# GpSimd scales the attention's probabilities, two kept products change places, four loads move behind the gMLP's tables

## The chip, the cores and the metric

The kernel runs on one core of a Trainium2 chip, as one program in one launch. The metric is the device time of one execution in microseconds; less is better. The core's engines work side by side, each through its own queue in order: TensorE (PE, matmuls; PEld, its weight loads), VectorE (DVE), ScalarE (ACT), GpSimd (POOL) and SyncE (SP). Transfers are issued from the queues of SP, ACT and POOL.

## The reference

One layer of a decoder trunk, in float32, with 512 positions and a width of 2048:

```
h = rms_norm(x, norm_g)
q, kv, g_logits, z_a, uv, z_b, merge_logits = split(h @ w_in)     # w_in is 2048 x 10800
o_a = nsa_attention(q, ...) * silu(z_a)           # 16 heads of 64, 4 key/value groups
o_b = spatial_gating(uv, ln_v_g, ln_v_b, sgu_w, sgu_b) * silu(z_b)
g_a, g_b = split(sigmoid(merge_logits))
x = x + (g_a * (o_a @ w_up_a) + g_b * (o_b @ w_up_b)) @ w_out
x = x + sigmoid(x @ w_ple_gate) * (p @ w_ple)
return rms_norm(x, final_g)
```

The attention has three branches, each with its own keys and values and a sigmoid gate per head and position: compressed, selected and windowed. With 512 positions the selection takes all 8 blocks and the window covers everything before the query, so the last two are plain causal attention with a linear bias per head:

```
o = gb[0] * o_c + gb[1] * o_s + gb[2] * o_w        # o_s = softmax(q k_s * scale - slope * distance) v_s
```

`spatial_gating` computes `u * (tril(W_s) LN(v) + b)` in chunks of 128 positions and 8 groups, with `uv = gelu(uv)`; `b` is `sgu_b`, `W_s` is `sgu_w`.

## The kernel before

Every float32 operand of a matmul is split into a high part, a copy rounded by ScalarE (`high`, L156 and L158), and a low part, the rest, by VectorE (`low`, L162 and L164); a product is three matmuls (high by high, high by low, low by high). Weight tiles arrive through SP's queue (`raw`, `b11`, `b12`, `more`) and are split into `hi` and `lo`, or `hs` and `ls`.

A generator `gemm` runs through a list of jobs in order: `pl` (embedding), `kw`, `vw`, `q0`, `q1`, the block jobs `kv`, `u`, `vn`, `zb` and `m0` to `m3`, the `q` and `za` jobs, `ub0`, `ub1`, `ua0`, `ua1`, and then `wo` and `pg`. `fill(n)` lets it issue n more units, `finish(name)` all up to the end of a job. At each step of a job it calls `flush()`, which issues what was deferred, splits weights two steps ahead, and `pop()`, which issues the next items of a list called `background`. So the order of every queue is fixed by the order in which the program issues.

A block job (kind "S") computes a block of output with seven block products, named by digits, instead of eight. They come in the order 1 and 5 in turn, 6 and 3 in turn, 7, 2 and 4 in turn. One step is 12 matmuls. Products 1, 6, 7 and 4 go to one pair of PSUM banks, 5 and 3 to a second, 2 to a third. `evac_quad` empties them: after products 1, 5 and 6 ScalarE copies the pair to two SBUF tiles (`keep`, L635); after 3, 7 and 2 VectorE adds the kept tiles (`keep6`, `keep5`, `keep1`) and `final` is called on the sum; after 4 `final` takes the banks themselves. The tiles come from rings: `s1` has two, `hi` four, `lo` three. In the `ub` jobs `final` multiplies by the gate (L756) and stores the tile to `y_dram` from GpSimd's queue (L763); the tile is free when the store has landed.

The block jobs over `h` need sums of its parts. The "third sums" of product 7 are written to `s3_dram` during the first jobs, and `load_s3` (L1114) brings them with four transfers of 512 KB from GpSimd's queue to the places in `act_h` and `act_l` that product 7 reads. It stands directly behind `finish("q1")`, ahead of the block job `kv`. The first background item of that job is `load` of `sgu_items`: from the same queue it loads `sgu_b` (`bn`, L1123) and `sgu_w` (`wn`, two transfers, L1126), makes a triangular mask (L1128, L1129) and copies `ln_g` and `ln_b` to DRAM (L1132). Five items later TensorE transposes `bn` (`bias`, L1136), then `wn` (L1143).

The attention is software-pipelined over 48 slots: for each of eight pairs of heads (`ft`) two for query block 3, two for block 2 and one each for blocks 1 and 0. In period s the program issues

- `scores(s)`: TensorE multiplies (L1518, L1519); VectorE adds the bias and takes the extreme of each row (L1522); the exponentials with their sums follow on ScalarE, deferred (L1531),
- `weigh(s - 1)`: VectorE inverts the sums (L1540), multiplies by the branch's gate (L1542) and scales the probabilities with the result (L1546), one instruction for each head and branch: two or four, 128 in all,
- `transpose_probs(s - 2)`: TensorE transposes them (L1570), and ScalarE and VectorE split the result into `pth` and `ptl`,
- `values(s - 3)`: TensorE multiplies by the values (L1589, L1590); `fold` adds the halves, the last addition and the product with the gate on GpSimd (L1607, L1609),

with units of the `q` and `za` jobs between them. The compressed branch of a group of heads (`cmp_scores`, `cmp_softmax`, `cmp_weigh`, `cmp_transpose`, `cmp_values`) and transfers on GpSimd's queue (`load_ob`, L1681 to L1684; `add_half`, L1688) are spread over the periods. `evac_za` multiplies by the gate path on GpSimd (L543).

Of the kernel before, what the change touches and what calls it, by code (L numbers as in the profile page):

```python
# [17 lines left out]
ALU = mybir.AluOpType  # L18
# [60 lines left out]
def kernel(ctx: ExitStack, tc: tile.TileContext, x, p, norm_g, w_in,  # L79
                      pe_k, w1_k, w2_k, pe_v, w1_v, w2_v, ln_g, ln_b, sgu_w, sgu_b,  # L80
                      w_up_a, w_up_b, w_out, w_ple, w_ple_gate, final_g, out):
    nc = tc.nc
    x, out = x[0], out[0]
    p = p[0, 0]
    norm_g, w_in, ln_g, ln_b, sgu_w, sgu_b = norm_g[0], w_in[0], ln_g[0], ln_b[0], sgu_w[0], sgu_b[0]
    pe_k, w1_k, w2_k, pe_v, w1_v, w2_v = pe_k[0], w1_k[0], w2_k[0], pe_v[0], w1_v[0], w2_v[0]
    w_up_a, w_up_b, w_out, w_ple, w_ple_gate = w_up_a[0], w_up_b[0], w_out[0], w_ple[0], w_ple_gate[0]
# [3 lines left out]
    stream = ctx.enter_context(tc.tile_pool(name="stream", bufs=3))  # L91
# [3 lines left out]
    def bank(kind, name):  # L95
        return psum.tile([P, 512], F32, tag=kind, name=name)
# [164 lines left out]
    quad = {}  # L261
# [212 lines left out]
    def mtile(tag, shape, dtype, name):  # L474
        return mix["pool"].tile(shape, dtype, tag=tag, name=name, bufs=2 if tag == "v" else 1)
# [132 lines left out]
    def block(t, c):  # L608
        return slice(t * P, t * P + P), slice(c, c + 512)

    def later(f):
        deferred.append(lambda: deferred.append(f))
# [9 lines left out]
            return act_h(k, sl), act_l(k, sl)  # L622
        return sum_part(p, k, sl), sum_part(p, k, slice(t * P + 256, t * P + 256 + P))

    def evac_quad(final, place=None, tiles=True, minus=False, c21=None):


        keep = {}

        def e(p, ps):  # L630
            if p in "156":
                tag, pool, bufs = {"1": ("s1", quad["pool"], 2), "5": ("hi", stream, 4), "6": ("lo", stream, 3)}[p]
                keep[p] = [pool.tile([P, 512], F32, tag=tag, name="keep" + p, bufs=bufs) for _ in range(2)]
                for t in range(2):
                    nc.scalar.copy(keep[p][t], ps[t])  # L635
            elif p in "372":
                other, row, c = {"3": ("6", 0, 512), "7": ("5", 2, 512), "2": ("1", 0, 0)}[p]
                for t in range(2):
                    o = place(row + t, c) if place else keep[other][t]
                    if minus and c:  # L640
                        nc.vector.scalar_tensor_tensor(out=o, in0=ps[t], scalar=-1.0, in1=keep[other][t],
                                                       op0=ALU.mult, op1=ALU.subtract)
                    else:
                        nc.vector.tensor_tensor(out=o, in0=ps[t], in1=keep[other][t], op=ALU.add)
                    later(lambda o=o, t=t: final(row + t, c, o, o))
            else:
                for t in range(2):
                    o = place(2 + t, 0) if place else None
                    if c21:
                        o = c21(t)  # L650
                    elif tiles and not place:
                        o = stream.tile([P, 512], F32, tag="hi", name="c21", bufs=4)
                    final(2 + t, 0, o, ps[t])
        return e
# [29 lines left out]
    def final_u(t, c, o, src):  # L684
        nc.scalar.activation(o, src, AF.Gelu_apprx_tanh)
        nc.gpsimd.dma_start(u_dram[block(t, c)], o)

    block_job("kv", w_in, C_KV + 512, evac_quad(final_kv), c2=C_KV)
    for n, c, final in (("u", C_UV, final_u), ("vn", C_UV + 1024, final_vn), ("zb", C_ZB, final_zb)):
        block_job(n, w_in, c, evac_quad(final))  # L690
# [52 lines left out]
    def place(tag, dtype):  # L743
        return actp.tile([P, 4, S], dtype, tag=tag, name="p_" + tag)
# [10 lines left out]
    def gated(o, n, cg, t, src):  # L755
        nc.vector.scalar_tensor_tensor(out=o, in0=gate_tiles[n, cg][:, t], scalar=1.0, in1=src,  # L756
                                       op0=ALU.add, op1=ALU.mult)

    def final_ub(i):
        def f(t, c, o, src):  # L760
            cg = i + c // 256
            gated(o, 1, cg, t, src)
            later(lambda: nc.gpsimd.dma_start(y_dram[block(t, 512 * cg)], o))  # L763
        return f
# [18 lines left out]
    def make(name, w):  # L783
        m = {(n, j): dram.tile([256, 1024], F32, name=f"{name}{n}{j}_d") for n in "t7" for j in range(2)}

        def part(i, j):
            r, c = {"11": (0, 0), "12": (0, 1024), "21": (512, 0), "22": (512, 1024)}[i]
            return w[r + 256 * j:r + 256 * j + 256, c:c + 1024]
        for n, i in (("t", "11"), ("7", "22")):
            for j in range(2):  # L790
                made_copies.append((m[n, j], part(i, j)))
                made_adds.append((m[n, j], part("12", j)))

        def src(i):
            c = slice(512 * i, 512 * i + 512)
            return lambda n, j: (m[n, j] if n in "t7" else part(n, j))[:, c]
        return src
# [3 lines left out]
    def up_job(name, w, made, act, evac, banks):  # L801
        add_job(Job(name, "S", w, 0, 512, 8, act, evac, banks, made=made,
                    after=lambda p, j: after_up.get((name, p, j), nothing)()))

    made = make("ub", w_up_b)
    for i in range(2):
        up_job(f"ub{i}", w_up_b, made(i), ob_act, evac_quad(final_ub(i), minus=True), ("sto", "tos")[i])
    made = make("ua", w_up_a)
    for i in range(2):
        up_job(f"ua{i}", w_up_a, made(i), oa_act, evac_quad(final_ua(i), place_ua(i), minus=True), ("ost", "sto")[i])  # L810
# [188 lines left out]
    with tc.tile_pool(name="xin", bufs=4, side="right") as xin:  # L999
# [7 lines left out]
        st = xin.tile([P, TT, 2], F32, name="st", bufs=1)  # L1007
# [103 lines left out]
    def load_s3():  # L1111
        for q in range(2):
            for i, a in enumerate((act_h, act_l)):
                nc.gpsimd.dma_start(a(slice(4 * q, 4 * q + 4), hi_t), s3_dram[:, i, 4 * q:4 * q + 4])  # L1114

    load_s3()

    def sgu_items():
        w = {}

        def load():
            w["bn"] = quad["pool"].tile([8, P], F32, tag="s1", name="bn", bufs=2)
            nc.gpsimd.dma_start(w["bn"], sgu_b)  # L1123
            w["wn"] = [mtile("v", [P, 4, P], F32, "wn") for _ in range(2)]
            for hf in range(2):
                nc.gpsimd.dma_start(w["wn"][hf], sgu_w[4 * hf:4 * hf + 4].rearrange("g t s -> t g s"))  # L1126
            t = w["tri"] = mtile("w", [P, P], F32, "tri")
            nc.gpsimd.memset(t, 1.0)  # L1128
            nc.gpsimd.affine_select(out=t, in_=t, pattern=[[1, P]], compare_op=ALU.is_ge, fill=0.0,  # L1129
                                    base=0, channel_multiplier=-1)  # L1130
            for i, src in enumerate((ln_g, ln_b)):
                nc.gpsimd.dma_start(ln_dram[:, i], bass.AP(tensor=src.tensor, offset=src.offset, ap=[[0, P], [1, 1024]]))  # L1132

        def bias():
            b = bank("g", "ps_b")
            nc.tensor.transpose(b[:, :8], w["bn"], ident[:8, :8])  # L1136
            deferred.append(lambda: nc.vector.tensor_copy(sgu_bt, b[:, :8]))

        def mask(hf):
            def f():  # L1140
                b = bank("g", "ps_w")
                for j in range(4):
                    nc.tensor.transpose(b[:, j * P:j * P + P], w["wn"][hf][:, j], ident)  # L1143

                def store():
                    o = mtile(f"g{hf}", [P, 4, P], F32, "ws")
                    nc.vector.tensor_tensor(out=o, in0=b.rearrange("p (g t) -> p g t", g=4),
                                            in1=w["tri"].unsqueeze(1).to_broadcast([P, 4, P]), op=ALU.mult)
                    nc.gpsimd.dma_start(ws_dram[:, 4 * hf:4 * hf + 4], o)
                deferred.append(store)  # L1150
            return f
        return [load] + 4 * [nothing] + [bias, mask(0), mask(1), nothing]

    def w1_items():
        t = {}
# [168 lines left out]

    pe_items, kv_items = conv_items()
    background.extend(sgu_items() + w1_items() + pe_items)
    state["pops"] = 1
    finish("kv")
# [207 lines left out]
    def weigh(s):  # L1536
        ft, i, br = slots[s]
        n, nb = (i + 1) * P, len(br)
        pts, st = prob[s]
        nc.vector.reciprocal(st[:, 1, :nb], st[:, 1, :nb])  # L1540
        gv = gates[:, i].rearrange("p (b h) -> p b h", b=3)[:, 1 + br[0]:1 + br[0] + nb, 2 * ft:2 * ft + 2]
        nc.vector.tensor_tensor(out=st[:, 0, :nb], in0=st[:, 1, :nb], in1=gv, op=ALU.mult)  # L1542
        for hh in range(2):
            for j in range(nb):
                sl = pts[hh][:, j * n:j * n + n]
                nc.vector.tensor_scalar(out=sl, in0=sl, scalar1=st[:, 0, j, hh:hh + 1], scalar2=None, op0=ALU.mult)  # L1546

    def blocks(s):
        ft, i, br = slots[s]
# [136 lines left out]
    def add_half(i):  # L1686
        o, src = made_adds[i]
        nc.gpsimd.dma_start(o, src, accum_op=ALU.add, max_dma_last_dim=4096)  # L1688

    off_pe = (cmp_keys, cmp_weigh, weigh, load_ob, add_half)  # L1690
    cmp_keys(0)
    nc.gpsimd.dma_start(vt, v_dram)
# [6 lines left out]
    for s in range(n + 3):  # L1699
        events = []  # L1700
        if s < n:
            ft, j = slots[s][0], s % 6
            events.append((scores, s))
        if 1 <= s <= n:
            events.append((weigh, s - 1))
# [357 lines left out]
```

## Time and profile before

| | us |
|---|---|
| median of 3 runs | 1549.9 |
| lowest and highest of them | 1546.38, 1551.77 |
| the profiled execution, time | 1550.63 |
| its span, first to last instruction | 1548.9 |

| engine | busy us | share of the span | instructions |
|---|---|---|---|
| PE | 1524.1 | 98% | 7270 |
| DVE | 1232.0 | 80% | 1901 |
| ACT | 821.6 | 53% | 1379 |
| POOL | 294.4 | 19% | 457 |

A row of a group of instructions gives line, engine, operation, output from inputs, and counts. A row of waits gives who waited for whom, then us in total, times, and the longest. A row of the timeline gives the start in us from the span's start, the duration of the merged instructions, engine, line, operation and count, and in brackets the idle time before it and what ended it. A row of windows gives the stretch, its length, busy time and instructions of each engine, the clock granted to TensorE (1.00 is full speed), and the DMA engines' share and rate. All times come from one profiled execution.

### The profile page before, as it was taken

How to read it: one execution, taken by the hardware profiler on the slowest of the kernel's cores; microseconds unless marked ns; L12 is line 12 of the kernel's file. 1: busy time of each engine (PE TensorE's matmuls, PEld its weight loads, DVE VectorE, ACT ScalarE, POOL GpSimd, SP SyncE). 2: the span in 40 equal slices, each digit the busy share in tenths (PEclk: the TensorE clock that was granted, in tenths of full speed). 3: DMA queues.
4: the chain of work that ended last, by engine and by line, in shares of the span. 5: the costliest groups of instructions: out<-in, count | busy, mean ns of one | idle time of the engine just before them, and what ended most of it. 6: DMA issues, size and time to landing. Idle time of an engine off the chain costs nothing.

```text
span 1548.9 us, 20363 instructions
## 1 busy us (share of the span) xinstructions
PE 1524.1 (98%) x7270; PEld 1267.5 (82%) x7270; DVE 1232.0 (80%) x1901; ACT 821.6 (53%) x1379; POOL 294.4 (19%) x457
## 2 busy tenths in 40 slices
PE   9999999999999999999999999999999999999997
PEld 7887888888888888888788878887788888888885
DVE  7787877777889788888488888968887498988877
ACT  6454445444455555555466666655555244544556
POOL 2232343321021111113112121231121121100000
PEclk9999999999999999999999999999999999999999
DMA  9896979672548575769734344547686588554565
GB/s 324 216 300 185 266 110 265 184 243 86 196 159 236 184 250 178 240 238 295 201 72 107 68 96 97 107 170 271 219 286 156 150 243 259 155 199 169 185 207 187
DMA packets 189941, 300.43 MB, mean 194 GB/s; under 512 B 29912, under 2 KB 94080, under 8 KB 188048
## 3 DMA queue, kind: packets, MB, share of 16 engines
q1 hardware_dynamic: 107088, 153.77, 31.4%
q0 software_dynamic: 75824, 128.32, 30.3%
q10 hardware_dynamic: 6928, 17.04, 3.2%
q8 instruction: 57, 0.93, 0.2%
q14 instruction: 44, 0.36, 0.1%
HBM read 235.25 MB, written 81.66 MB: 205 GB/s over the span
## 4 chain that ended last, share of the span: by engine, by line
PE 87%; DVE 5%; issue 4%; ACT 2%; DMA 1%; POOL 1%; ACTq 0%; DVEq 0%; POOLq 0%
PE ps_m L362 6%; PE ps_m L363 6%; PE ps_m L361 6%; PE ps_t L1570 2%; PE ps_za L392 2%; PE ps_wo L403 2%; PE ps_za L390 2%; PE ps_za L391 2%; PE ps_wo L402 2%; PE ps_wo L404 2%; PE ps_u L361 2%; PE ps_zb L361 2%; PE ps_vn L361 2%; PE ps_u L363 2%; PE ps_vn L363 2%
## 5 line engine op out<-in xcount | busy, mean ns | idle before, releaser
L162 DVE TENSOR_TENSOR ls<-b,hs 128x1024 fp32r<-128x1024 f32 x200 | 244.5, 1224 | 118.4 <-ACT hs L156 117.3
L156 ACT CAST hs<-b 128x1024 fp32r<-128x1024 f32 x200 | 209.8, 1052 | 226.8 <-PE ps_m L363 50.1
L156 ACT CAST hs<-raw 128x1024 fp32r<-128x1024 f32 x104 | 109.5, 1053 | 108.7 <-PE ps_m L363 25.3
L162 DVE TENSOR_TENSOR ls<-raw,hs 128x1024 fp32r<-128x1024 f32 x104 | 127.8, 1229 | 28.9 <-ACT hs L156 28.6
L162 DVE TENSOR_TENSOR lo<-raw,hi 128x512 fp32r<-128x512 f32 (+1 forms) x152 | 101.9, 674 | 49.8 <-PE ps_wo L403 22.2
L156 ACT CAST hi<-raw 128x512 fp32r<-128x512 f32 (+1 forms) x152 | 89.2, 601 | 61.5 <-PE ps_wo L404 34.9
L362 PE MATMUL ps_m<-ls,act_h 128*128 128x512 f32 x256 | 99.7, 390 | 0.5 <-DVE ls L162 0.5
L361 PE MATMUL ps_m<-hs,act_h 128*128 128x512 f32 x256 | 100.2, 391 | 0.0
L363 PE MATMUL ps_m<-hs,act_l 128*128 128x512 f32 x256 | 99.7, 389 | 0.0
L288 DVE TENSOR_TENSOR b<-b,b 128x1024 f32<-128x1024 f32 x80 | 97.5, 1219 | 0.1
L288 DVE TENSOR_TENSOR b<-raw,b 128x1024 f32<-128x1024 f32 x80 | 97.5, 1218 | 0.0
L1531 ACT ACTIVATE prob<-prob,st 128x512 f32<-128x512 f32 (+3 forms) x128 | 70.7, 555 | 21.4 <-DVE st L1522 21.3
L156 ACT CAST pth<-ps_t 128x512 fp32r<-128x512 f32 (+1 forms) x88 | 47.6, 543 | 45.5 <-PE ps_t L1570 45.0
L162 DVE TENSOR_TENSOR ptl<-ps_t,pth 128x512 fp32r<-128x512 f32 (+1 forms) x88 | 55.6, 639 | 19.2 <-ACT pth L156 18.8
L1522 DVE CUSTOM_DVE_ANT_0 prob<-ps_s,b 128x512 f32<-128x512 f32 (+3 forms) x128 | 56.4, 487 | 8.7 <-PE ps_s L1519 8.0
L156 ACT CAST hs<-more 128x1024 fp32r<-128x1024 f32 x32 | 33.7, 1054 | 45.4 <-DVE more L283 18.2
L362 PEld LDWEIGHTS ps_m<-ls,act_h 128*128 128x128 f32 x256 | 48.1, 188 | 10.7 <-DVE ls L162 0.9
L363 PEld LDWEIGHTS ps_m<-hs,act_l 128*128 128x128 f32 x256 | 48.1, 188 | 10.0
L361 PEld LDWEIGHTS ps_m<-hs,act_h 128*128 128x128 f32 x256 | 48.1, 188 | 9.8
L390 PE MATMUL ps_za<-act_h,hi 128*128 128x512 f32 x128 | 54.6, 427 | 0.0
L1570 PEld LDWEIGHTS ps_t<-ident,prob 128*128 128x128 f32 x320 | 39.5, 141 | 18.1 <-DVE ptl L162 5.3
L390 PE MATMUL ps_q<-act_h,hi 128*128 128x512 f32 x128 | 54.4, 425 | 0.0
(675 smaller groups left out, 4486.6 us busy)
## 6 DMA issues: line engine op xcount, KB each, us to landing
raw<-in_w_in_dram SPq DMA_DIRECT2D x100, 512.0 KB, 4.5
b<-in_w_in_dram SPq DMA_DIRECT2D x64, 512.0 KB, 6.2
raw<-in_w_out_dram SPq DMA_DIRECT2D x24, 512.0 KB, 4.1
raw<-in_w_ple_gate_dram SPq DMA_DIRECT2D x24, 512.0 KB, 3.9
gate<-keep ACTq DMA_DIRECT2D x24, 256.0 KB, 5.8
raw<-in_w_up_b_dram SPq DMA_DIRECT2D x12, 512.0 KB, 7.9
raw<-in_w_up_a_dram SPq DMA_DIRECT2D x12, 512.0 KB, 5.0
xt<-in_x_dram SPq DMA_DIRECT2D x4, 1024.0 KB, 9.6
```

What stands on the lines that cost most here:

```text
L156: nc.scalar.copy(hi, src)
L162: nc.vector.tensor_tensor(out=lo, in0=src, in1=hi.bitcast(F32), op=ALU.subtract)
L288: nc.vector.tensor_tensor(out=b[o], in0=b[x], in1=b[y], op=ALU.subtract)
L361: nc.tensor.matmul(o, ah, hi[:, i], start=st, stop=False, skip_group_check=go)
L362: nc.tensor.matmul(o, ah, lo[:, i], start=False, stop=False, skip_group_check=go)
L363: nc.tensor.matmul(o, al, hi[:, i], start=False, stop=sp, skip_group_check=go)
L390: nc.tensor.matmul(ps, hi[:, j], ah, start=st, stop=False)
L391: nc.tensor.matmul(ps, hi[:, j], al, start=False, stop=False)
L392: nc.tensor.matmul(ps, lo[:, j], ah, start=False, stop=sp)
L1522: nc.vector.tensor_tensor_reduce(out=pt[:, j * n:j * n + n], in0=o[:, j], in1=b0[:, 512 - n:], scale=-SLOPE[h], scalar=3.0e38, op0=ALU.add ...
L1531: nc.scalar.activation(sl, sl, AF.Exp, bias=st[:, 0, j, hh:hh + 1], scale=-1.0, accum_out=st[:, 1, j, hh:hh + 1])
L1570: nc.tensor.transpose(b[:, (2 * e + hh) * P:(2 * e + hh + 1) * P], pts[hh][:, c:c + P], ident)
```

## The change

Three things. The scaling of the probabilities in `weigh` is issued on GpSimd instead of VectorE; the inversion and the gate stay. `evac_quad` gets a switch, used for `ub1` alone: keep1 then takes the `hi` tiles and keep5 the `s1` tiles. And `load_s3` is no longer called ahead of the `kv` job; it is the second background item in it, behind `load` of `sgu_items`, in place of an empty one. Its later call in the output projection stays where it is.

```diff
-    def evac_quad(final, place=None, tiles=True, minus=False, c21=None):
+    def evac_quad(final, place=None, tiles=True, minus=False, c21=None, swap=False):
...
-                tag, pool, bufs = {"1": ("s1", quad["pool"], 2), "5": ("hi", stream, 4), "6": ("lo", stream, 3)}[p]
+                tag, pool, bufs = {"15"[swap]: ("s1", quad["pool"], 2), "51"[swap]: ("hi", stream, 4), "6": ("lo", stream, 3)}[p]
...
-        up_job(f"ub{i}", w_up_b, made(i), ob_act, evac_quad(final_ub(i), minus=True), ("sto", "tos")[i])
+        up_job(f"ub{i}", w_up_b, made(i), ob_act, evac_quad(final_ub(i), minus=True, swap=i == 1), ("sto", "tos")[i])
...
-    load_s3()
-
     def sgu_items():
...
-        return [load] + 4 * [nothing] + [bias, mask(0), mask(1), nothing]
+        return [load, load_s3] + 3 * [nothing] + [bias, mask(0), mask(1), nothing]
...
-                nc.vector.tensor_scalar(out=sl, in0=sl, scalar1=st[:, 0, j, hh:hh + 1], scalar2=None, op0=ALU.mult)
+                nc.gpsimd.tensor_scalar(out=sl, in0=sl, scalar1=st[:, 0, j, hh:hh + 1], scalar2=None, op0=ALU.mult)
```

## The prediction

> **What bounds the kernel now.** I read the page first, then the waits of TensorE, then windows around its waits, then single rows in order of time.
>
> ```profile
> span 1548.9 us, 20363 instructions
> PE 1524.1 (98%) x7270; PEld 1267.5 (82%) x7270; DVE 1232.0 (80%) x1901; ACT 821.6 (53%) x1379; POOL 294.4 (19%) x457
> ```
> ```profile
> PE ps_t L1570 <- DVE ptl L162: 2.8, 2, 2.5
> PE ps_ub L361 <- ACT keep L635: 2.5, 2, 1.8
> PE ps_c L1662 <- DVE st L1522: 2.0, 1, 2.0
> PE ps_b L1136 <- DMA bn<-in_sgu_b_dram: 1.2, 1, 1.2
> PE ps_t L1570 <- DVE prob L1546: 0.8, 1, 0.8
> PE ps_c L1672 <- DVE st L1522: 0.2, 1, 0.2
> ```
> ```profile
> 770.00:1030.00 260.00, 254.01 (x1427) 213.44 (x1426) 221.61 (x673) 172.57 (x464) 47.78 (x72) 0.99 0.40 91
> 844.00:850.00 6.00, 6.00 (x26) 5.05 (x27) 5.89 (x22) 2.85 (x8) 0.80 (x2) 0.72 0.08 13
> 915.00:921.00 6.00, 5.20 (x23) 4.60 (x24) 4.11 (x21) 3.85 (x14) 0.00 (x0) 0.72 0.00 0
> ```
>
> TensorE is busy 98% of the span. Nothing in the change takes work from it, so all that can be won are its waits (us in total, times, longest) and the time it runs at a lower clock. The waits shown are 9.5 us. Four of the six rows lie in the attention (770 to 1030 us, the windows' columns being PE, PEld, DVE, ACT, POOL, granted clock, DMA share, GB/s): 2.8 + 2.0 + 0.8 + 0.2 = 5.8 us. Its two long waits are each followed by 6 us at a mean granted clock of 0.72, which loses 6 x 0.28 = 1.7 us twice. So the attention loses 5.8 + 3.4 = 9.2 us. The 1.8 us wait lies in the second up block, the 1.2 us wait at the gMLP's bias. Each part of the change meets one of these three places.
>
> **Part 1: the scaling goes to GpSimd.** It takes this off VectorE, 128 instructions, and puts 128 on GpSimd:
>
> ```profile
> 770.00:1030.00 260.00, 43.08 (x128) 0.99 0.40 91
> ```
>
> VectorE falls from 221.6 to 178.5 us of 260. The trace has no multiplication by a per-partition scalar on GpSimd. The nearest rows:
>
> ```profile
> L1655 POOL TENSOR_TENSOR cs<-cs,cst x4: 1049/1052/1282, 760.9 to 975.3; 128x512 f32<-128x512 f32 x4
> 726.63 1.59 POOL L1468 TENSOR_SCALAR_AFFINE_SELECT b<-b 128x512 f32<-128x512 f32 x1
> 726.53 1.22 DVE L288 TENSOR_TENSOR b<-raw,b 128x1024 f32<-128x1024 f32 x1
> 727.71 1.58 DVE L162 TENSOR_TENSOR ls<-raw,hs 128x1024 fp32r<-128x1024 f32 x1
> L162 DVE TENSOR_TENSOR lo<-raw,hi x45: 675/684/1018, 771.9 to 1028.1; 128x512 fp32r<-128x512 f32 x45
> ```
>
> The two-input operation takes 1.05 us. The one-input select took 1.59, but VectorE's operation with two SBUF inputs had started 0.1 us before it, at 726.53, and ended at 727.75. The select then needed 728.22 - 727.75 = 0.47 us, and VectorE's next one, normally 1.22, took 1.58 until the select was out of its way. So the two engines shut each other out; a one-input operation of 512 columns costs 0.47 alone and up to 1.59 shut out. Between 0.47 and 1.05 I take 0.6, nearest the row with one input. All 40,960 columns per partition (80 of such 512) then add 48 us, or 84 at 1.05, to GpSimd's 47.8 of 260: it doesn't fill. What VectorE pays back: its 45 `lo` of 0.68 us meet a busy GpSimd some 40% of the time and wait half of 0.6, 45 x 0.4 x 0.3 = 5 us of the 43.
>
> The Trainium skill, "GPSIMD Engine Reference", section 3.1, gives 769 ns for 512 elements in the best loop; by that the two late groups below would cost 0.3 us more each and the gain be 0.7 us less.
>
> What counts is the time from the start of a group's scaling to the transposes that read it. The first group, a late one, and a usual one:
>
> ```profile
> 772.88 0.88 DVE L1546 TENSOR_SCALAR prob<-prob,st 128x512 f32<-128x512 f32 x2
> 773.43 0.94 PE L1570 MATMUL ps_t<-ident,prob 128*128 128x128 f32 x4 [0.78 <-DVE prob L1546]
> 868.78 0.88 DVE L1546 TENSOR_SCALAR prob<-prob,st 128x512 f32<-128x512 f32 x2
> 869.43 0.84 PE L1570 MATMUL ps_t<-ident,prob 128*128 128x128 f32 x4
> 899.04 0.89 DVE L1546 TENSOR_SCALAR prob<-prob,st 128x512 f32<-128x512 f32 x2
> 901.97 0.60 PE L1570 MATMUL ps_t<-ident,prob 128*128 128x128 f32 x4
> ```
>
> There are 0.55, 0.65 and 2.93 us. On GpSimd a pair takes 1.2 instead of 0.88, so the first two cost 0.3 us each, the third nothing. For the first, VectorE was not in arrears; its 0.8 us wait becomes 1.1. Elsewhere the start comes earlier by what VectorE is relieved of, about 0.9 us a group. GpSimd's queue is in order: ahead of a group may stand the output adds, the gate products, the four loads of `load_ob` and the accumulating copy of `add_half`. They wait for work of an earlier step, and the loads are issued in the step before; behind the scaling stand the same, which nobody waits for at once.
>
> The two long waits:
>
> ```profile
> 843.91 0.66 PE L1570 MATMUL ps_t<-ident,prob 128*128 128x128 f32 x4 [2.46 <-DVE ptl L162]
> 830.00:844.00 14.00, 13.44 (x32) 1.00 0.57 114
> 830.00:844.00 14.00, 1.77 (x4) 1.00 0.57 114
> 910.67 0.40 PE L392 MATMUL ps_q<-act_h,lo 128*128 128x512 f32 x1
> 911.50 1.19 ACT L158 ACTIVATE qs<-ps_q 64x512 fp32r<-64x512 f32 x2
> 912.73 1.39 DVE L164 SCALAR_TENSOR_TENSOR qs<-ps_q,qs 64x512 fp32r<-64x512 f32 x2 [0.21 <-ACT qs L158]
> 915.80 0.63 PE L1662 MATMUL ps_c<-ident,cs 128*128 128x128 f32 x4 [1.99 <-DVE st L1522]
> ```
>
> Ahead of the first, VectorE was busy 13.44 of 14 us (first window), 1.77 of them scaling (second). Without it `ptl` comes up to 1.8 earlier: 2.46 becomes 0.7. The second hangs on a chain: ScalarE copies q at 911.50, VectorE follows at 912.73 after waiting 0.21 for it. TensorE had finished q at 911.07, so the chain can start only 0.43 earlier: 1.99 becomes 1.6. Waits of 1.84 and less show no low clock behind them in this trace, so I count both 1.7 us of low clock as gone. After: 1.1 + 0.3 + 0.7 + 1.6, and 0.5 for the two small waits (0.3 and 0.2), is 4.2, plus 0.4 for `lo` shut out at a bad moment: 4.6. Gain 9.2 - 4.6 = 4.6 us; bounds: 9.2 - 1.1 = 8.1 with every other wait gone, and below nothing (the rivals).
>
> **Part 2: keep1 and keep5 change places in the second up block.** No instruction is added.
>
> ```profile
> 1075.14 1.10 POOL L763 DMA_DIRECT2D y_d<-keep  x2
> 1082.63 1.14 POOL L763 DMA_DIRECT2D y_d<-keep  x2
> 1091.06 0.59 ACT L635 COPY keep<-ps_ub 128x512 f32<-128x512 f32 x1 [3.39 <-DMA y_d<-keep]
> 1089.24 0.39 PE L362 MATMUL ps_ub<-ls,ob_h 128*128 128x512 f32 x1
> 1089.47 0.39 PE L363 MATMUL ps_ub<-hs,ob_l 128*128 128x512 f32 x1
> 1091.70 0.50 PE L361 MATMUL ps_ub<-hs,p_l 128*128 128x512 f32 x1 [1.84 <-ACT keep L635]
> ```
>
> ScalarE waits 3.39 us to copy keep1, because the `s1` tile still goes to DRAM as the first block's keep1 (stored at 1082.63, its last product). TensorE waits 1.84 for the bank. Changed, keep1 takes the `hi` tiles of the first block's keep5, stored at 1075.14, 7.5 us earlier, so it finds them free: gain 1.8 us. keep5 now waits for the `s1` tiles, until about 1091.1 and 1092.0; its bank is next needed by product 3, a step (12 matmuls, 0.23 us apart by the rows, 2.8 us) after product 6 starts at 1089.9, so at 1092.6 and 1093.3. The copies of 0.59 end by 1091.7 and 1092.6: hidden with 0.7 to spare. Queued behind ScalarE's wait is the cast for the step after, which starts at 1092.6 as before and is needed with its `ls` at 1095.4. Without that cover the cost would be the 1.8 again. In the first ua block keep1's `s1` comes free earlier and keep5's `hi` one product later: nothing.
>
> **Part 3: the third sums' loads go behind the tables.**
>
> ```profile
> 111.05 0.76 POOL L1114 DMA_DIRECT2D act_h<-s_d  x1
> 114.55 0.58 POOL L1123 DMA_DIRECT2D bn<-in_sgu_b_dram  x1
> 123.08 0.20 PE L1136 MATMUL ps_b<-ident,bn 8*128 8x8 f32 x1 [1.21 <-DMA bn<-in_sgu_b_dram]
> L635 ACT COPY keep<-ps_kv x6: 587/589/593, 128.8 to 151.8; 128x512 f32<-128x512 f32 x6
> ```
>
> Four loads of 0.76 us stand before `bn` on GpSimd's queue. Behind it they let `bn` start 3 us earlier (111.5); even with the 8.5 us to 123.08 it lands at 120, before the transpose could run at 123.08 - 1.2 = 121.9: gain 1.2 us. The loads move past five DMAs, a memset and a select on that queue and one step of the background work, some 4 us; product 7, which reads them, starts after the last keep at 151.8, more than 25 us later. SP's queue isn't touched. `wn` and the weight mask also come earlier.
>
> **Sum.** 4.6 + 1.8 + 1.2 = 7.6 us off the profiled 1550.6 (span 1548.9): 1543.0. That execution was 0.7 above the median of the runs shown, 1549.9, so 1542.3 against it; I say 1542.5.
>
> **Rivals.** *The attention's waits form anew.* TensorE's waits there hang on the chain scores, exponentials, q copies as well as on VectorE's load; the 0.21 row speaks for it, the 13.44 of 14 against. Then only parts 2 and 3 count: 1549.9 - 3.0 = 1546.9, no change that can be told; differences under 0.3% (4.6 us) can't. *GpSimd is too slow and it gets slower.* Place: the scaling of the long groups. At the shut-out 1.59 per operation a pair takes 3.2 us; against the mean of the three starts shown, 1.4, plus 0.9 of relief, each of the 16 pairs is 0.9 us late: 14.4, with two spells of low clock 17.8. That is 8.6 more than now, less 3.0: 1555.5. It turns slower when the pairs lose 12.2 us, 0.76 each, at 1.53 us per operation. Against it: only 45 `lo` stand against 128 scalings. *A first call is dear.* A first use of this operation that takes 6 us would stop TensorE once, and with 1.7 us of low clock cost 7.7: 1550. The first of GpSimd's four two-input products took 1.28, the others 1.05, so the trace speaks against it. The rule is that of the Trainium skill, "GPSIMD Engine Reference", section 2.1: some 6 us for the first call of a freshly loaded kernel.
>
> **How the numbers follow.** Forecast 0.59 (own range 1538.5 to 1546; 0.54 of it faster by over 0.3%, below 1545.3); waits form anew 0.25 (0.03 faster, 0.22 same); too slow 0.12; dear first call 0.04 (same). With 0.05 of the forecast in "same": faster 0.57, same 0.31, slower 0.12. The range leaves out the outer part of the slow case and of the best: 1537.5 to 1553.
>
> **What would show it.** Right: VectorE near 183 us between 770 and 1030; GpSimd's scaling at 0.5 to 0.8 us for 512 columns; no wait of 2 us at ps_t or ps_c and no window at 0.72; no ps_ub wait of 1.8, none for `bn`. Wrong: many waits of ps_t for GpSimd's prob, `lo` much over 0.7 us, or a low clock at the attention's start. A pair over 2.5 us would make the forecast wrong.

## The result, and the profile after: slower by 0.6%

The changed kernel takes 1557.27 us (median of 5 runs, 1556.41 to 1558.36), the kernel before 1548.52 (5 runs beside it, 1546.38 to 1551.77): a ratio of 1.0058, 95% interval [1.0047, 1.0069]. The forecast was 1542.5, faster. The profiled execution took 1557.26, so it stands for the median.

The head of the page, then TensorE's waits and the largest wait of its weight loads:

```profile
span 1555.1 us, 20573 instructions
PE 1526.7 (98%) x7270; PEld 1267.5 (82%) x7270; DVE 1196.0 (77%) x1773; ACT 822.2 (53%) x1379; POOL 432.7 (28%) x585
```
```profile
PE ps_t L1568 <- POOL prob L1544: 10.3, 11, 2.0
...
PE ps_t L1568 <- DVE ptl L162: 1.2, 1, 1.2
...
PE ps_ub L361 <- ACT keep L635: 0.8, 1, 0.8
...
PE ps_c L1660 <- DVE st L1520: 0.4, 1, 0.4
```
```profile
PEld ps_t L1568 <- POOL prob L1544: 17.8, 23, 2.5
```

The waits that the forecast started from have shrunk or gone: `ptl` 2.8 to 1.2, `ps_c` 2.0 to 0.4, the keep 2.5 to 0.8, no `bn`, no DVE prob. (`ps_t` is the bank of the transposes, `ps_c` one of the compressed branch.) One row that was not there before outweighs them: the transposes wait 11 times for GpSimd's probabilities, 10.3 us. The scaling (L1544; weigh's product by the gate is now L1540, the transposes L1568) by shape, then the attention's stretch, all instructions and the scaling alone:

```profile
L1544 POOL TENSOR_SCALAR prob<-prob,st 128x512 f32<-128x512 f32 x32 | 51.8, 1672 | 20.7 <-DVE st L1540 12.3 <-ACT prob L1529 4.1 <-PE ps_s L1517 3.3
L1544 POOL TENSOR_SCALAR prob<-prob,st 128x384 f32<-128x384 f32 x32 | 40.1, 1264 | 28.2 <-DVE st L1540 21.4 <-ACT prob L1529 3.5 <-PE ps_t L1568 1.7
L1544 POOL TENSOR_SCALAR prob<-prob,st 128x256 f32<-128x256 f32 x32 | 29.6, 944 | 12.6 <-ACT prob L1529 6.3 <-DVE st L1540 6.2
L1544 POOL TENSOR_SCALAR prob<-prob,st 128x128 f32<-128x128 f32 x32 | 19.2, 623 | 11.7 <-ACT prob L1529 8.8 <-DVE st L1540 2.8
```
```profile
770.00:1030.00 260.00, 248.28 (x1385) 206.42 (x1383) 180.75 (x537) 168.18 (x456) 182.49 (x196) 0.99 0.40 88
770.00:1030.00 260.00, 139.48 (x126) 0.99 0.40 88
```

An instruction of 512 columns takes 1.67 us on average (median 1.57); by the medians (0.61, 0.93, 1.25 and 1.57) each 128 columns add 0.32 us. All 128 make 141 us, not 48. VectorE did fall, from 221.6 to 180.75, and GpSimd is not full (182 of 260). The time went where a pair is late. The attention's first group, and the clock behind the two worst places:

```profile
771.20 0.16 DVE L1540 TENSOR_TENSOR st<-st,kvg 128x2 f32<-128x2 f32 x1
771.58 3.12 POOL L1544 TENSOR_SCALAR prob<-prob,st 128x512 f32<-128x512 f32 x2 [9.05 <-DVE st L1540]
773.21 0.33 PE L1568 MATMUL ps_t<-ident,prob 128*128 128x128 f32 x1 [2.05 <-POOL prob L1544]
774.76 0.90 PE L1568 MATMUL ps_t<-ident,prob 128*128 128x128 f32 x3 [1.22 <-POOL prob L1544]
```
```profile
774.00:780.00 6.00, 5.24 (x23) 4.54 (x24) 2.26 (x4) 2.89 (x7) 4.81 (x4) 0.72 0.63 101
876.50:882.00 5.50, 5.50 (x25) 4.71 (x24) 3.93 (x8) 3.25 (x9) 3.93 (x3) 0.69 0.95 158
```

The factor is ready at 771.36 and GpSimd starts 0.22 us later. TensorE waits 2.05 us for head 0, transposes it, and waits 1.22 more for head 1. Then it runs 6 us at a mean clock of 0.72, as before behind two waits elsewhere: the low clock was not removed, it moved to 774 and 876.

How much this costs is safer read from the starts of TensorE's instructions than from its idle time, since the ends are modelled. From the first score to the first product of the up blocks the starts span 274.65 us before and 283.51 after, 8.9 more. The steps that lead to a transpose take 51.2 before and 63.1 after, 11.9 more, and 11.6 of that lies between one transpose and the next of the same tile, whose four alternate between head 0 and head 1: it is head 1, second in GpSimd's queue, that is late. The rest of the attention gained 3.0.

One stage outside the attention is longer too. From the first product of the output projection `wo` to the first of `pg` it is 173.19 us before and 174.53 after. ScalarE waits there for a store that lands later, before and after:

```profile
1259.38 0.59 ACT L156 CAST x2t<-ps_x 128x512 fp32r<-128x512 f32 x1 [1.43 <-DMA x2t_d<-x2t]
```
```profile
1265.81 0.59 ACT L156 CAST x2t<-ps_x 128x512 fp32r<-128x512 f32 x1 [3.46 <-DMA x2t_d<-x2t]
```

No instruction of that stage was changed. The stage takes 174.3 to 174.8 us in the profiled executions of all six kernels here that do all 128 products of the probabilities on GpSimd, and 173.2 in all others. Why the store lands later stays open.

### The profile page after: what moved, and what is told of

It reads as the page before. It is cut to its first block, busy times and chain, and to the rows that moved or that the text cites. A ratio compares the mean times of both kernels' runs of the same rounds, so it can differ in the third digit from the quotient of the medians.

```text
span 1555.1 us, 20573 instructions
## 1 busy us (share of the span) xinstructions
PE 1526.7 (98%) x7270; PEld 1267.5 (82%) x7270; DVE 1196.0 (77%) x1773; ACT 822.2 (53%) x1379; POOL 432.7 (28%) x585
## 4 chain that ended last, share of the span: by engine, by line
PE 87%; DVE 6%; ACT 3%; POOL 2%; issue 2%; DMA 1%; ACTq 0%; DVEq 0%; POOLq 0%
PE ps_m L362 6%; PE ps_m L363 6%; PE ps_m L361 6%; PE ps_t L1568 2%; PE ps_u L361 2%; PE ps_kv L361 2%; PE ps_zb L361 2%; PE ps_vn L361 2%; PE ps_u L363 2%; PE ps_kv L362 2%; PE ps_vn L363 2%; PE ps_u L362 2%; PE ps_vn L362 2%; PE ps_ua L362 2%; PE ps_ua L363 2%
## 5 line engine op out<-in xcount | busy, mean ns | idle before, releaser
L1544 POOL TENSOR_SCALAR prob<-prob,st 128x512 f32<-128x512 f32 (+3 forms) x128 | 140.7, 1126 | 73.2 <-DVE st L1540 42.6
L1568 PE MATMUL ps_t<-ident,prob 128*128 128x128 f32 x320 | 54.7, 281 | 11.9 <-POOL prob L1544 10.3
L1568 PEld LDWEIGHTS ps_t<-ident,prob 128*128 128x128 f32 x320 | 40.2, 143 | 29.6 <-POOL prob L1544 17.8
```

The lines of the kernel that those rows point to most:

```text
L1544: nc.gpsimd.tensor_scalar(out=sl, in0=sl, scalar1=st[:, 0, j, hh:hh + 1], scalar2=None, op0=ALU.mult)
L1568: nc.tensor.transpose(b[:, (2 * e + hh) * P:(2 * e + hh + 1) * P], pts[hh][:, c:c + P], ident)
```

## The experiments

Each kernel's ratio is against the kernel before, measured beside it on the same chip. Differences between kernels that were measured at different times are less sure; where much hangs on one, the difference of the two ratios stands beside it.

**The change taken apart.** Scaling back on VectorE, parts 2 and 3 kept:

```diff
-                nc.gpsimd.tensor_scalar(out=sl, in0=sl, scalar1=st[:, 0, j, hh:hh + 1], ...)
+                nc.vector.tensor_scalar(out=sl, in0=sl, scalar1=st[:, 0, j, hh:hh + 1], ...)
```

> Parts 2 and 3 without part 1: VectorE scales the probabilities again. If the loss is all part 1's (the theory: an operation of GpSimd costs 1.57 us for 512 columns, and its groups come late to the transposes), the attention takes as long as before, the up blocks and the gMLP's bias keep their gains, and the time is 3 to 4 us below before: about 1545. If parts 2 and 3 lose something that the changed kernel's trace hides (the output projection ran 1.3 us longer there), it is 1548 or more.

Part 1 alone, `evac_quad` and `load_s3` as before:

> Part 1 alone. Theory: the attention alone loses 8.9 us as in the changed kernel's trace, so with the up blocks' and the bias's waits back the time is 1559 to 1561, some 3 us above the changed kernel. Rival (the three parts disturb one another, part 1 alone is not at fault): at or below 1553.

Parts 2 and 3: 1545.41 us, 0.9974 [0.9964, 0.9984], 4.1 us off. Part 1: 1560.8, 1.0075 [1.0062, 1.0088], 11.3 us on. Both as expected; together they make 7.1 of the 8.8. In the first kernel the attention's two long waits stay as they were, so parts 2 and 3 do nothing there:

```profile
PE ps_t L1568 <- DVE ptl L162: 2.8, 2, 2.5
PE ps_c L1660 <- DVE st L1520: 2.0, 1, 2.0
```

**The duration of GpSimd's instruction.** The same product, on GpSimd, in the form with two inputs (the factor spread along the row):

```diff
-                nc.gpsimd.tensor_scalar(out=sl, in0=sl, scalar1=st[:, 0, j, hh:hh + 1], ...)
+                nc.gpsimd.tensor_tensor(out=sl, in0=sl, in1=st[:, 0, j, hh:hh + 1].to_broadcast([P, n]), op=ALU.mult)
```

> The changed kernel, but GpSimd scales with its two-input product, the factor spread over the columns, instead of the product by a per-partition scalar. Theory of the price: this form took 1.05 us for 512 columns in the trace before, a pair then takes 2.1 to 2.2 us instead of 3.1, and about half of the waits of TensorE for GpSimd's probabilities go: 1550 to 1553. Rival (the two engines shut each other out of the memory port): a form that reads two operands holds the port no less, VectorE's 0.68 us operations grow, and the time stays at 1556 or rises.

It took 1550.61, 1.0009 [1.0000, 1.0018]. The rows of the 512-column scaling and of the wait:

```profile
L1544 POOL TENSOR_TENSOR prob<-prob,st 128x512 f32<-128x512 f32 x32 | 34.1, 1104 | 27.3 <-DVE st L1540 17.3 <-PE ps_s L1517 3.3 <-ACT pth L156 3.1
```
```profile
PE ps_t L1568 <- POOL prob L1544: 5.6, 10, 1.5
```

The form with two inputs is the shorter one (median 1.04 against 1.57), the wait falls from 10.3 to 5.6 and the kernel gains 6.7 us. Yet here VectorE's weight splits `lo` are shut out more (825 ns on average, 754 in the changed kernel, 705 before). So it isn't their being shut out that makes most of the loss.

**More time for the pair inside the period.** The values of step s - 3 are issued ahead of the transposes of step s - 2:

```diff
-        events += tq[:1] + vq[:1]
+        events += vq[:1] + tq[:1]
...
-        events += tq[1:] + vq[1:]
+        events += vq[1:] + tq[1:]
```

> The changed kernel, but in each period of the attention the product with the values is issued ahead of the transposes instead of behind them, so that each group's scaling has one event more (about 1.2 us) before TensorE needs it; GpSimd's work, its price and its neighbours stay the same. Theory (lateness): the waits for GpSimd's probabilities, 10.3 us over 11 times, fall below 3 and the time to 1549 to 1552. Rival (shut-out and load, not lateness): the time stays above 1555.

1557.05, 1.0052 [1.0038, 1.0066]: the expectation missed. The wait halves, and a new one takes its place:

```profile
PE ps_o L1588 <- DVE ptl L162: 5.1, 7, 1.9
PE ps_t L1568 <- POOL prob L1544: 4.7, 4, 2.0
```

The transposes start later, so `pth` and `ptl` do, and the values of the next period wait for them. From scores to values there is a fixed number of slots; slack can be moved within it, not made.

**What the scaling is worth at most.** It is left out (the probabilities stay unscaled):

```diff
-                nc.gpsimd.tensor_scalar(out=sl, in0=sl, scalar1=st[:, 0, j, hh:hh + 1], ...)
+                pass
```

> The changed kernel with the scaling of the probabilities left out altogether (its output lacks the softmax's division and the gates of two branches): VectorE has its 43 us back and nobody does the work. This bounds what the relief of VectorE can bring in the attention, against 1545.4 of parts 2 and 3 alone. The prediction's view of the two long waits (2.46 to 0.7, 1.99 to 1.6, no low clock behind them): 5 to 7 us less, 1538.5 to 1540.5. Rival (the waits hang on the chain through TensorE and ScalarE, VectorE's load hardly counts): 1543.5 or more.

1541.81, 0.9955 [0.9942, 0.9968], between the two expectations. Against the 1545.4 with the scaling on VectorE, taking all of it away wins 3.6 us (2.9 by the two ratios): that is what moving it could bring at best. And the first long wait, which the forecast put down to VectorE's load, is still there. VectorE and TensorE ahead of it:

```profile
836.59 0.41 DVE L1603 TENSOR_TENSOR fold<-fold,ps_o 64x256 f32<-64x256 f32 x1 [1.04 <-issue]
...
837.47 0.69 DVE L1650 TENSOR_REDUCE cst<-cs 128x16 f32<-128x512 f32 x1
...
838.48 0.69 DVE L1652 TENSOR_TENSOR cst<-cst,kvg 128x16 f32<-128x16 f32 x1
839.21 1.39 DVE L164 SCALAR_TENSOR_TENSOR qs<-ps_q,qs 64x512 fp32r<-64x512 f32 x2
840.63 0.69 DVE L162 TENSOR_TENSOR ptl<-ps_t,pth 128x512 fp32r<-128x512 f32 x1
841.37 0.66 PE L1568 MATMUL ps_t<-ident,prob 128*128 128x128 f32 x4 [2.38 <-DVE ptl L162]
```

VectorE stood idle for 1.04 us shortly before, so it was not in arrears. What delays `ptl` is what the program issues ahead of it: the sum, the inversion and the gate product of the compressed branch (`cmp_weigh`) and two q copies, 3.2 us from 837.47 to the start of `ptl`. In the trace before the same work stands directly ahead of that `ptl`.

**Half of it on GpSimd.** Head 0 is scaled on VectorE, head 1 on GpSimd, first in the changed kernel's form, then in the form with two inputs:

```diff
+                (nc.gpsimd if hh else nc.vector).tensor_scalar(out=sl, in0=sl, scalar1=st[:, 0, j, hh:hh + 1], ...)
```

> The changed kernel, but VectorE scales the first head of each group and GpSimd the second, by the same operation. VectorE is relieved of 21 us, GpSimd's share of a pair is one operation of 1.57 + 0.2 us, begun beside VectorE's. Theory (what counts is how long a group takes from the factor to the last product): 1.8 us stands between VectorE's 0.9 (1545.4) and the two-input pair's 2.1 to 2.3 (1550.6), so 1546 to 1549. Rival (it is the total load or the shut-out of the two engines): with 70 us on GpSimd, half of the changed kernel's, half of its loss of 12: 1551.

```diff
+                if hh:
+                    nc.gpsimd.tensor_tensor(out=sl, in0=sl, in1=st[:, 0, j, 1:2].to_broadcast([P, n]), op=ALU.mult)
+                else:
+                    nc.vector.tensor_scalar(out=sl, in0=sl, scalar1=st[:, 0, j, 0:1], ...)
```

> As the last, with GpSimd's half in the two-input form (1.05 us for 512 columns): a pair takes 1.25 us, 0.4 more than on VectorE, and VectorE is relieved of 21 us. Theory: the lateness costs under 1 us and the relief shortens the two long waits: 1542 to 1545, the best so far. Rival (relief is worth nothing): 1545.5 to 1547.

They took 1546.51, 0.9989 [0.9980, 0.9997], and 1543.51, 0.9967 [0.9955, 0.9980]: both times as expected. But the relief hardly shortened the two long waits, as the second expectation had it: in the second kernel they are 2.4 and 1.8. The scaling and the wait for it, of the first and of the second:

```profile
L1544 POOL TENSOR_SCALAR prob<-prob,st 128x512 f32<-128x512 f32 x16 | 28.2, 1760 | 27.3 <-DVE st L1540 11.2 <-ACT prob L1529 7.1 <-PE ps_t L1568 4.2
```
```profile
PE ps_t L1568 <- POOL prob L1544: 2.6, 3, 1.1
```
```profile
L1545 POOL TENSOR_TENSOR prob<-prob,st 128x512 f32<-128x512 f32 x16 | 20.0, 1250 | 31.3 <-DVE st L1540 19.3 <-ACT pth L156 4.1 <-PE ps_s L1517 3.3
```
```profile
PE ps_t L1571 <- POOL prob L1545: 1.1, 2, 0.6
```

Time follows the duration of the pair: 1.25 us gives 1543.5, 1.76 gives 1546.5, two at 1.04 give 1550.6, two at 1.57 give 1557.3. (VectorE's own pair of 0.88, in the kernel with parts 2 and 3 alone, gives 1545.4 and stands outside this row; VectorE is not relieved there.) The second kernel is the fastest here that computes everything. Against parts 2 and 3 alone (1545.41, measured at another time) it is 1.9 us less, and the intervals of the two ratios overlap.

**Is it the reading of the factor?** A constant in place of the factor (the probabilities are halved instead of scaled), one run:

```diff
+                nc.gpsimd.tensor_scalar(out=sl, in0=sl, scalar1=0.5, scalar2=None, op0=ALU.mult)
```

> The changed kernel with a constant 0.5 in place of the per-partition factor (its probabilities are not normalised), to see the price of the operation: if reading the factor makes it dear, 512 columns fall from 1.57 to 0.6 us or less, near the select's 0.47; if the operation itself is slow, they stay at 1.4 to 1.57 and the span within 2 us of the changed kernel's 1555.1.

```profile
L1544 POOL TENSOR_SCALAR prob<-prob 128x512 f32<-128x512 f32 x30 | 48.3, 1665 | 0.6 <-ACT prob L1529 0.6
```
```profile
PE ps_t L1568 <- POOL prob L1544: 0.6, 1, 0.6
```

The instruction is nearly as long (median 1.51), so the factor isn't the reason. The expectation for that case missed the span, though: 1546.4, not within 2 us of 1555.1. The time was 1548.15: the product no longer waits for the factor, starts right behind the exponentials, and hardly anyone waits for it, with GpSimd busy 176 us of the same 260.

**Load without lateness.** The scaling is left out, and in place of each instruction GpSimd does products that nobody reads:

```diff
-                nc.gpsimd.tensor_scalar(out=sl, in0=sl, scalar1=st[:, 0, j, hh:hh + 1], ...)
+                for _ in range(n // P):
+                    nc.gpsimd.tensor_scalar(out=pad_r, in0=b0[:, :56], scalar1=st[:, 0, j, hh:hh + 1], ...)
```

> The changed kernel with the scaling left out (so the probabilities are not normalised) and, in the place of each of the 128 instructions, one small product on GpSimd for each 128 columns, 56 columns wide, of a constant tile with the factor, into a tile that nobody reads: about 320 x 0.43 us = 137 us of GpSimd, as much as the scaling takes, starting at the same factor, but no transpose waits for it. Theory (the scaling is late for the transposes; its mere presence on GpSimd costs little): within about 2 us of the kernel without scaling, 1541.8, so at most 1544.5, with no wait of TensorE for prob. Rival (GpSimd's load costs by itself, since it shuts VectorE out of its two-input operations or delays the other work of its queue): 1550 or more, with longer `lo` and waits of ps_t for ptl.

1542.47, 0.9964 [0.9952, 0.9977]. The added products, the stretch of the attention, and the wait of the transposes:

```profile
L1545 POOL TENSOR_SCALAR pad_r<-b,st 128x56 f32<-128x56 f32 x320 | 154.1, 481 | 52.8 <-DVE st L1540 26.3
```
```profile
770.00:1030.00 260.00, 255.11 (x1448) 215.25 (x1447) 184.19 (x547) 172.88 (x464) 198.58 (x395) 1.00 0.43 96
```
```profile
PE ps_t L1569 <- DVE ptl L162: 1.9, 1, 1.9
```

GpSimd does 154 us of such work, more than the 141 of the changed kernel, and is busy 198.6 of 260, but the time stays within 0.7 us of the kernel without scaling (1.4 by the two ratios). GpSimd's busy time as such costs next to nothing. These products are short (median 0.42 us), so the length of an instruction was still open. The constant factor again, timed:

> The kernel with a constant of 0.5 in place of the factor once more, timed (the probabilities are halved instead of scaled; one run gave 1548.15). Its products on GpSimd have their full length, 1.5 us for 512 columns, but start right behind the exponentials, and in the run before TensorE waited for prob only 0.6 us. If lateness is all that costs, the time is within 3 us of the kernel without scaling, 1541.8, so at most 1545, and the single run was a high one. If instructions of that length cost something by themselves (VectorE shut out for longer than by the short ones of the kernel with idle load: `lo` 783 ns against 702), it stays at 1546.5 to 1549.5.

1546.56, 0.9982 [0.9973, 0.9991]: at the lower edge of the second case, 4.1 us above the kernel with idle load, though TensorE waits for prob only 0.7 us. The long wait for `ptl` is longer in it, 3.5 instead of 2.4 without scaling, and a low clock follows. Ahead of it a `lo`, normally 0.68 us, takes 1.53 beside GpSimd's products:

```profile
PE ps_t L1568 <- DVE ptl L162: 3.5, 1, 3.5
```
```profile
843.50:849.50 6.00, 6.00 (x28) 0.73 0.14 31
```
```profile
834.24 1.53 DVE L162 TENSOR_TENSOR lo<-raw,hi 128x512 fp32r<-128x512 f32 x1
```

So of the 14.8 us between the changed kernel (1557.3) and the one with idle load (1542.5), 10.7 go when the result is ready sooner, and the other 4.1 stay with long instructions that are hardly waited for. By the ratios the two shares are 11.8 and 2.8, the second uncertain by some 2.4. Lateness is the larger part. The smaller one is not the price of long instructions as such: between the profiled executions, which are 5.2 us apart, 1.45 lies in the output projection (174.66 against 173.21), and the execution with the constant has two spells of low clock, worth 3.4, where the one with idle load has none. That the `lo` causes the longer wait is read from the order of events, not tried.

**The order ahead of `ptl`.** `cmp_weigh` one slot later, first in the half-and-half kernel with two inputs, then with all scaling on VectorE:

```diff
-            if ft % 2 == 0 and ft > 0 and j in (1, 2, 4):
-                events.append(({1: cmp_softmax, 2: cmp_weigh, 4: cmp_transpose}[j], ft // 2))
+            if ft % 2 == 0 and ft > 0 and j in (1, 3, 4):
+                events.append(({1: cmp_softmax, 3: cmp_weigh, 4: cmp_transpose}[j], ft // 2))
```

> The kernel with head 0 scaled on VectorE and head 1 on GpSimd as a two-input product (1543.5), with the weighing of the compressed branch (VectorE's sum, reciprocal and product of the factors, and GpSimd's four products) issued one slot later, j = 3 instead of j = 2. Theory (the wait of 2.4 us of ps_t for ptl comes from what stands ahead of ptl in VectorE's queue at that slot, and not from VectorE's load): that wait shrinks to under 1 us, and the time is 1540.5 to 1543. Rival (it is the load, or another neighbour in the slot): the wait stays at 2 us or more, and the time at 1543 to 1545; a new wait of ps_c for the moved products, which now stand one slot closer to their transposes, would make it 1544 to 1547.

> Parts 2 and 3 with all scaling on VectorE (1545.4), with the weighing of the compressed branch issued one slot later, as in the run before. Theory: the wait of 2.8 us of ps_t for ptl shrinks to under 1 us although VectorE keeps all its load, and the time falls to 1542 to 1544.5. Rival (VectorE's arrears make it): the wait stays, 1545 to 1546.5.

The first took 1544.37, 0.9970 [0.9960, 0.9980], the second 1544.59, 0.9971 [0.9961, 0.9980]. TensorE's rows of the second:

```profile
PE ps_c L1660 <- DVE st L1520: 2.2, 1, 2.2
...
PE ps_t L1568 <- DVE ptl L162: 1.3, 2, 1.0
PE ps_c L1660 <- POOL vcb L1665: 1.1, 1, 1.1
...
PE ps_c L1660 <- POOL cs L1654: 0.9, 1, 0.9
```

With VectorE's load unchanged (222.5 us of 260) the 2.5 us wait for `ptl` falls to 1.0; in the first it falls from 2.4 to 0.9. So the order made most of it. Nothing is won in time: the products that moved stand closer to their transposes, and `ps_c` now waits 1.1 for `vcb` (the compressed branch's values, copied on GpSimd) and 0.9 for `cs` (its weighed probabilities). Both times missed the theory's range, the second by 0.1; for the first it is the third case, a new wait of `ps_c` (0.7 for `cs`).

## Why the prediction was wrong, point by point

- **The step that failed is the price of GpSimd's product: 0.6 us for 512 columns, measured 1.57** (0.62, 0.94 and 1.26 for 128, 256 and 384 columns, on average). The first pair takes 3.12 us instead of 1.2, and TensorE waits 10.3 us for such pairs where the forecast had 1.4. The bounds, 0.47 and 1.05, both missed it: they came from a select with one input and a product with two, and a product by a per-partition factor behaves like neither. One input does not mean cheaper: with two inputs the same product takes 1.04. The Trainium skill, "GPSIMD Engine Reference", section 3.1, has 769 ns for 512 elements at best, and its section 4.1 calls operations with one input roughly line-rate; the trace has 1.57 us against VectorE's 0.44 (half of its pair), and the measurement decides.
- **"Elsewhere the start comes earlier by what VectorE is relieved of, about 0.9 us a group"** did not hold either. From the end of a group's exponentials to its factor VectorE takes 4.29 us before and 4.29 after, on average over the 48 groups, and 4.16 with no scaling at all. Relief of all 43 us is worth the 3.6 us above in the whole kernel.
- **The first long wait, 2.46 to 0.7 by VectorE's load**: wrong reason. It is 2.38 without any scaling and 1.0 with all of it once `cmp_weigh` is moved. A window at 13.44 of 14 us says that an engine is busy, not that what it does first could have been later. In the changed kernel the wait fell to 1.17; that TensorE's own halts just ahead gave VectorE the time is argued, not shown.
- **The second long wait, 1.99 to 1.6**: it is 1.33 with no scaling, 1.8 with half of it on GpSimd, and 0.4 in the changed kernel. No experiment tells why.
- **Both spells of low clock gone**: they moved, and the loss stayed the same. The forecast judged by the length of a wait alone; where the wait falls counts too (last section).
- **VectorE pays back 5 us**: `lo` rose by 49 ns on average over 43 of them, 2 us.
- **Part 3, 1.2 us**: right. `bn` is issued at 112.14 and its transpose no longer waits; between the start of the `kv` job and the products of the gMLP behind it the profiled execution gained 1.25.
- **Part 2, 1.8 us**: about right. The two up blocks gained 2.4 us, of which 1.7 is the wait for keep, 2.5 to 0.8. ScalarE still waits for stores, but shorter ones, 0.60 and 0.75, and TensorE's 1.84 is gone:

```profile
1098.24 0.59 ACT L635 COPY keep<-ps_ub 128x512 f32<-128x512 f32 x1 [0.60 <-DMA y_d<-keep]
1099.57 0.59 ACT L635 COPY keep<-ps_ub 128x512 f32<-128x512 f32 x1 [0.75 <-DMA y_d<-keep]
```

Parts 2 and 3 together were put at 3.0; the kernel with these alone gained 4.1, and its interval, 2.5 to 5.6 us, holds 3.0.
- **The rival "GpSimd is too slow", 1555.5 at 1.59 us per operation**, came true in place and nearly in price and time, with luck in both. Its 1.59 was a select held up by VectorE, while 1.57 is the product's usual duration. And two errors of its sum cancelled: the 0.9 us of relief did not come, and not all 16 pairs are late for TensorE, which waits 11 times. Its break-even of 1.53 us was too generous. It has that relief in it, and it leaves out the 3.4 us of low clock that the rival's own sum counts; with them it would be 1.43. Measured, at 1.04 the attention already takes 277.9 us, 3.2 more than before, and only parts 2 and 3 bring the kernel back to even. "A pair over 2.5 us would make the forecast wrong": it is 3.1.
- **The rival "a first call is dear"** did not appear: the first pair on GpSimd takes 3.12 us, twice the usual 1.57, and starts 0.22 us behind its factor.
- **What a right price would have given**: where the pair takes 1.25 us (half on each engine), the price of the forecast's pair of 1.2, the kernel takes 1543.5, 1 us above the forecast. That kernel is not the same change, and its terms are not the forecast's: the long waits stay at 2.4 and 1.8, and no low clock follows them in its profiled execution. The form with two inputs, the same change otherwise, takes the 8.8 us of loss down to even. Both speak for the price as what decides the sign.

## What to carry to other kernels

Work that moves to a slower engine is priced by its latency to the next reader, not by the load it takes or adds: find the group whose reader waits soonest, and count the whole pair there (10.7 us here, against 4.1 that stay with long instructions hardly waited for, and about 1 for busy time). Where the trace lacks the exact kind of instruction, the nearest rows are no bounds; measure that kind first, or keep the range open above. And before a wait is put down to an engine's load, look for idle time on that engine just ahead of it: if there is some, it was not in arrears, and the order of its queue is the first suspect. None is no proof of the contrary: the trace before had no such pause ahead of the first long wait, and moving `cmp_weigh` a slot later still cut it from 2.5 to 1.0 with all scaling on VectorE.

## What the runs showed of the hardware

- GpSimd multiplies 512 columns by a per-partition factor in 1.57 us, by a constant in 1.51, and by a spread second input in 1.04 (medians).
- With VectorE scaling the other head at the same moment, the same two forms on GpSimd take 1.76 and 1.25 us, some 0.2 more. The Trainium skill, "SBUF — State Buffer", section "SBUF: two separate sides", has the two engines share a pair of ports under an exclusive lock; in the first group VectorE's scaling (0.49 us) still runs for 0.30 and 0.36 us when GpSimd's has begun, so some 0.2 us more is of the size that this would give, but no run here isolates the lock.
- The length of a wait alone doesn't decide whether a low clock follows. The windows (TensorE's busy time and its clock) behind a wait of 2.38 us without scaling, and of 2.45 us with parts 2 and 3 alone:

```profile
841.40:847.40 6.00, 6.00 (x36) 1.00 0.09 19
```
```profile
842.90:848.90 6.00, 6.00 (x26) 0.72 0.06 9
```

In the same 6 us there are 36 matmuls in the one and 26 in the other. What differs is where the wait falls. Between the first 20 us and the end of the work every low spell in these traces lasts 3.41 us (one, in part 1 alone, twice that), and where a trace has two they begin a whole number of 3.41 us apart: before, 845.21 and 916.89, 21 of them. On that grid the wait of 2.45 us, from 840.42 to 842.87, lies inside one stretch, and the next one runs at half clock. The wait of 2.38, from 838.99 to 841.37, is cut by an edge into 1.29 and 1.09, and nothing follows:

```profile
839.47:842.88 3.41, 0.96 (x8) 1.00 0.31 95
842.88:846.29 3.41, 3.41 (x12) 0.50 0.00 0
```
```profile
836.87:840.28 3.41, 2.12 (x14) 1.00 0.62 174
840.28:843.69 3.41, 2.32 (x14) 1.00 0.00 0
```

In the attention and the up blocks of all 14 traces a low spell begins behind every such stretch in which TensorE idles more than 1.86 us and behind none with less than 1.70; between these both occur, and the ends of matmuls are modelled. The Trainium skill, "TensorE: Matmul & The Clock Gate", part 1, has the clock halved by windows of some 3.4 us that run on their own; the 3.41 us at 0.50 and the even spacing agree.
